# Head norms of both token tiles in two phases, and a new order of the memory's first norms, in a two-layer hybrid attention kernel

## The chip, the cores and the metric

The kernel runs on one core of a Trainium2 chip. The metric is the time of one execution on the device in microseconds, the median of several runs. Five engines work side by side: TensorE (PE, and PEld for its weight loads), VectorE (DVE), ScalarE (ACT), GpSimd (POOL) and SyncE (SP, which only issues DMAs).

## The reference

Two layers of attention on 256 tokens of width 1024, all in fp32. In each layer the rows of x are normed and multiplied by `w_in`, which gives queries, keys, values and gates of three branches: six heads of causal attention (the "a" columns; with 256 tokens its block selection falls away), six heads of dilated attention (the "b" columns) and four heads that look at 256 rows of a memory (the "m" columns). The memory's keys and values are the normed memory rows times `w_mem_kv`. Every head of queries and keys, 64 wide, is normed with a gain of its own; the a and b heads are also rotated by position:

```
qa = rope(rms_norm(to_heads(a_q), qk_g[0])); ka = rope(rms_norm(to_heads(a_k), qk_g[1]))
qb, kb: the same with qk_g[2], qk_g[3]
mkv = rms_norm(mem, mem_norm_g) @ w_mem_kv
qm = rms_norm(to_heads(m_q), qk_g[4]); km = rms_norm(to_heads(m_k), qk_g[5])
y = concat([oa * silu(a_g), ob * silu(b_g), om * silu(m_g)]);  x = x + y @ w_out
```

## The kernel before

**Tiling.** The 256 tokens (and the 256 memory rows) are two tiles of 128, t = 0 and 1. Every weight is brought from memory in fp32 into a buffer `raw` (three of these) and split into `hi`, a rounded copy (ACT, line 429), and `lo`, the rest (DVE, line 430), of which five each are held. Each product is three matmuls: hi·xmh, hi·xml, lo·xmh, where xmh and xml are the same split of the activations. A piece of a weight that is split at once is called a part; the parts are numbered from 0 in the order mkv (0 to 3), mq (4, 5), mg (6, 7), bq (8 to 11), bk (12 to 15) and so on. The variable `ahead` says how many parts beyond the one that is multiplied next are already split in program order.

**PSUM.** Four banks `acc` go round among the projections, two for each: mkv has the first two, mq the other two, mg the first two again, bq those of mq. A projection can start on a bank only when all that reads the one before it is done. Three banks `wk` serve transposes and scores, and one, `o`, the attention's output.

**Order.** The order of PE's instructions is written out by hand: a projection is a list of steps, and between them a small planner with a clock of estimated costs puts in the transposes, scores and outputs of heads that are due (`poll`, `spawn`; the `D_` constants are the delays that it plans with). While `pinning[0]` is set, which lasts from the start until the memory's keys of layer 0 are normed, DVE, ACT, POOL and the DMA queue keep program order too. After that the library's scheduler orders these engines by its own costs, with program order as the priority.

**The norm of heads** (`normed`, lines 256 to 276) takes one accumulator of one tile: ACT squares it (260), DVE sums over each head (262), DVE multiplies by 1/64 and adds epsilon (154), POOL raises to the power -1/2 (155), DVE multiplies the accumulator by the gain or by gain times cosine (266); for a and b DVE also multiplies the swapped halves by gain times sine (271) and adds (275); last, DVE multiplies by the head's factor (276). It is called for t = 0, then for t = 1, and each call ends before the next begins in program order.

**Layer 0 around the memory** (lines 553 to 579). mkv is computed from memory rows that carry no factor yet. After mq's first step ACT copies mkv to `kv`; after mq's fourth step the first memory tile's row factor is made (a Square over 1024 columns with a sum, ACT 160; DVE 154; POOL 155). At mq's first part the parts 6 and 7 are split, at its second part 8. Then come the norms of mq for both tiles, the second memory tile's row factor, two DMAs (the constants and the other gains), and for each tile a multiplication of `kv` by its row factor (573) and the norm of its keys. Line 515 multiplies the gain of the memory's queries, of both layers, by 0.125 on POOL. Then POOL makes the tables of gains times cosine and sine (203 to 208), PE runs mg, and bq follows. The transposes of the memory's queries and keys (PE, line 113) are planned into bq.

Of the kernel before, what the change touches and what calls it, by code (L numbers as in the profile page):

```python
# [25 lines left out]
SPLIT_BUFS = 5  # L26
# [40 lines left out]
def hybrid_kernel(ctx: ExitStack, tc: tile.TileContext, x, mem, mem_t, gains, w_in, w_out, w_mem_kv, qk_g, const, out):  # L67
    nc = tc.nc
    cp = ctx.enter_context(tc.tile_pool(name="cp", bufs=1))
    wp = ctx.enter_context(tc.tile_pool(name="wp", bufs=2))  # L70
    sp = ctx.enter_context(tc.tile_pool(name="sp", bufs=2))
# [17 lines left out]
    def pin(ins):  # L89

        return tc.keep_in_program_order(ins) if pinning[0] else ins
# [142 lines left out]
    def project_t(xs, chunk, n):  # L234

        accs = [acc_p.tile([P, 512], F32, tag="acc", name="acc")[:, :T] for _ in range(n // P)]

        def steps():
            for k0, nk, w in chunk:
                for k in range(nk):  # L240
                    products([(acc, k0 + k, [x[:, k0 + k] for x in xs], [p[:, k, e * P:(e + 1) * P] for p in w])
                              for e, acc in enumerate(accs)], 0, KD - 1, x_moves=True)
                    yield

        return accs, steps()

    def run(projection):
        accs, steps = projection
        for _ in steps:
            poll()  # L250
        return accs

    def heads(v):
        return v.rearrange("p (h d) -> p h d", d=HD)

    def normed(acc, n, dst, tables):

        h = n // HD
        sq = sp.tile([P, n], F32, tag="sq", name="sq", bufs=2)
        pin(nc.scalar.activation(sq, acc, AF.Square))  # L260
        ss = sp.tile([P, h], F32, tag="hss", name="hss", bufs=4)
        pin(nc.vector.tensor_reduce(ss, heads(sq), axis=AX.X, op=ALU.add))  # L262
        rs = sp.tile([P, h], F32, tag="hrs", name="hrs", bufs=4)
        rsqrt(rs, ss, h, 1.0 / HD)
        t1 = sp.tile([P, n], F32, tag="t1", name="t1", bufs=2)
        pin(nc.vector.tensor_tensor(heads(t1), heads(acc), tables[0][:, None, :].to_broadcast([P, h, HD]),
                                    op=ALU.mult))
        if len(tables) > 1:
            t2 = sq
            half = dict(s=2, d=HD // 2)  # L270
            pin(nc.vector.tensor_tensor(t2.rearrange("p (h s d) -> p h s d", **half),
                                        acc.rearrange("p (h s d) -> p h s d", **half)[:, :, ::-1, :],
                                        tables[1].rearrange("p (s d) -> p s d", s=2)[:, None]
                                        .to_broadcast([P, h, 2, HD // 2]), op=ALU.mult))
            pin(nc.vector.tensor_tensor(t1, t1, t2, op=ALU.add))
        pin(nc.vector.tensor_tensor(heads(dst), heads(t1), rs.unsqueeze(2).to_broadcast([P, h, HD]), op=ALU.mult))  # L276

    live = dict(pr=0, pT=0, o=0, heads=0, pairs=0, s=0, t=0, v=0)

# [84 lines left out]
    for side in "ab":  # L364
        c = in_cols[side + "g"][0]
# [69 lines left out]
    def weights():  # L435

        i = at[0]
        at[0] += 1
        while at[1] < len(splits) and units[splits[at[1]][0]][0] == i:
            s = at[1]  # L440
            at[1] += 1
            split(s + ahead[0])
            yield splits[s][1], splits[s][2], parts[s]
# [37 lines left out]
    for l in range(DEPTH):  # L481
# [3 lines left out]
        if l == 0:  # L485

            mem_xs = xm_tiles()
            first = sp.tile([P, WHOLE, T], F32, tag="v", name="whole", bufs=2)
            mkv, steps = project(mem_xs, weights(), 512)
            r_mem = []  # L490
            g = gT[:, 16:24]
            for k in range(WHOLE):

                whole[k] = first[:, k]
                pin(nc.vector.tensor_scalar(whole[k], memT[:, k], g[:, k:k + 1], None, op0=ALU.mult))
                next(steps)
            for k2 in range(WHOLE, KD - 2, 2):
                split_x(mem_xs, memT[:, k2:k2 + 2], g, k2)
                split(k2 // 2 + 1)
                next(steps)  # L500
            turned = [(o_p.tile([P, 2 * T], F32, tag="o", name="o") if k2 == 6 else work()).rearrange(
                "p (a t q) -> p a t q", a=2, t=NT) for k2 in range(0, KD, 2)]
            for t in range(NT):
                normed_rows(t, xn)
                for k in range(KD):
                    transpose(turned[k // 2][:, k % 2, t], xn[:, t, k * P:(k + 1) * P])
            split_x(mem_xs, memT[:, KD - 2:KD], g, KD - 2)
            split(KD // 2)
            next(steps)
            for k2, v in zip(range(0, KD, 2), turned):  # L510
                split_x(xs, v.rearrange("p a t q -> p a (t q)"), gx, k2)
                if k2 < 4:
                    split(SPLIT_BUFS + k2 // 2)
            mem_gain = gB[:, :, 4]
            pin(nc.gpsimd.tensor_scalar(mem_gain, mem_gain, 0.125, None, op0=ALU.mult))
            ahead[0] = SPLIT_BUFS - 1
        else:
            mkv, steps = project(mem_xs, weights(), 512)
            for t in range(NT):
                normed_rows(t, xn)  # L520
            for k in range(KD):
                next(steps)
                if k >= KD // 2:
                    split_x(xs, transposed(xn, 2 * k - KD), gx, 2 * k - KD)
# [4 lines left out]
        def gates(accs, dst):  # L529
            for e, acc in enumerate(accs):  # L530
                th = sp.tile([P, T], F32, tag="th", name="th", bufs=2)
                nc.scalar.activation(th, acc, AF.Tanh, scale=0.5)
                nc.vector.scalar_tensor_tensor(dst[:, e], th, 1.0, acc, op0=ALU.add, op1=ALU.mult)
# [23 lines left out]
        for i, _ in enumerate(steps):  # L557
# [4 lines left out]
            if i == 3 and l == 0:  # L562
                mem_junk = sp.tile([P, D], F32, tag="v", name="mem_junk", bufs=2)
                r_mem.append(row_scale(mem_sb, 0, "rmem", mem_junk))
        for t, acc in enumerate(mq):
            normed(acc, 256, qn[:, t], [gB[:, l, 4]])
        if l == 0:
            r_mem.append(row_scale(mem_sb, 1, "rmem", mem_junk))
            pin(nc.sync.dma_start(cst, const))
            load_gains(0, 4)  # L570
        for t in range(NT):
            if l == 0:
                pin(nc.scalar.activation(kv[:, t], kv[:, t], AF.Copy, scale=r_mem[t]))
            normed(kv[:, t, 0:256], 256, kn[:, t], [gB[:, l, 5]])
        pinning[0] = False
        start_heads(2, 6, qn, kn, None, v, gate, ready, D_NORM + D_MEM)
        tab = prepare_tables(l)
        gates(run(project_t(xs, weights(), 256)), gate)
        ready["gate"] = clock[0] + D_EVAC

        for kind, e0 in ((2, 3), (0, 0)):
            if kind == 2:
                masks = [cst[:, C_DIL:C_DIL + 128], cst[:, C_DIL + 128:C_DIL + 384]]
            else:
                masks = [cst[:, C_CAUSAL + 128:C_CAUSAL + 256], cst[:, C_CAUSAL:C_CAUSAL + 256]]
            if l + 1 < DEPTH and kind == 0:
                mem_xs = xm_tiles()
                spawn(next_mem(mem_xs, gT[:, 24 + 8 * l:32 + 8 * l]), D_FIRST_MEM)
            qn, kn, v, gate = head_tiles(384, 384)
            ready = dict(v=1e9, gate=1e9)  # L590
            for i, dst in ((0, qn), (1, kn)):
                for t, acc in enumerate(run(project(xs, weights(), 384))):
                    normed(acc, 384, dst[:, t], (tab[:, kind + i, 0, t], tab[:, kind + i, 1, t]))
            start_heads(3, e0, qn, kn, masks, v, gate, ready)
            for t, acc in enumerate(run(project(xs, weights(), 384))):
                nc.scalar.copy(v[:, t], acc)
            ready["v"] = clock[0] + D_EVAC
            gates(run(project_t(xs, weights(), 256)), gate[:, 0:2])
            gates(run(project_t(xs, weights(), 128)), gate[:, 2:3])
            ready["gate"] = clock[0] + D_EVAC  # L600
# [64 lines left out]
```

## Time and profile before

| | |
|---|---|
| Runs | 294.54, 295.4 and 712.39 us; median 295.4 us |
| Profiled execution | 294.36 us, of which the span from the first to the last instruction is 292.6 us |
| Busy in the span | PE 285.8 us, PEld 250.6, DVE 204.3, ACT 200.0, POOL 53.8 |
| TensorE clock granted | full, in every slice |
| DMA | 47.33 MB, mean 162 GB/s |

A row of the timeline gives the start in us from the span's start, the time, the engine, the line, the operation, what it writes and reads, how many instructions were merged into the row, and in brackets how long the engine had been idle before, and what ended that. PE's ends are modelled, since matmuls are pipelined; their starts are what was recorded. ACT and DVE may start an instruction before the one ahead has ended.

### The profile page before, as it was taken

Reading aid. Unit: us, or ns where it says so; the run is one execution under the profiler, and the core shown is the slowest. Engines: PE = TensorE matmul, PEld = TensorE weight load, DVE = VectorE, ACT = ScalarE, POOL = GpSimd, SP = SyncE. Lnnn points to the kernel's source line nnn. Section 1 sums busy time; section 2 is a strip of 40 time slices with the busy share of each in tenths; the row PEclk is TensorE's granted clock in tenths of the full one; section 3 lists DMA queues with packets and bytes.
Section 4 is the critical chain, followed back from the end, with each engine's and each line's share of the span. In section 5 each row is a group of like instructions: output and inputs, shape, how many; then the busy total and the mean of one; then the engine's idle time right before and its main releaser. Section 6 shows DMA issues by size and latency. Waiting matters only on the chain.

```text
span 292.6 us, 4974 instructions
## 1 busy us (share of the span) xinstructions
PE 285.8 (98%) x1810; PEld 250.6 (86%) x1810; DVE 204.3 (70%) x456; ACT 200.0 (68%) x445; POOL 53.8 (18%) x73
## 2 busy tenths in 40 slices
PE   8999889999999999999999999999999999999994
PEld 5699879889988999877788999989899899987773
DVE  1696889796557997755585577979655699765413
ACT  2997858785798747978375655868588864698600
POOL 0103596030002130000011049703000123000000
PEclk9999999999999999999999999999999999999999
DMA  7999565609227046646106727560913715820003
GB/s 236 389 367 373 184 182 186 179 2 319 57 71 237 19 155 262 196 162 224 65 19 233 225 101 195 168 179 2 298 38 109 239 52 165 316 81 36 3 0 143
DMA packets 32793, 47.33 MB, mean 162 GB/s; under 512 B 1280, under 2 KB 27648, under 8 KB 32768
## 3 DMA queue, kind: packets, MB, share of 16 engines
q1 hardware_dynamic: 32336, 46.22, 48.5%
q10 hardware_dynamic: 432, 0.79, 0.8%
q8 instruction: 14, 0.23, 0.3%
q14 instruction: 11, 0.09, 0.1%
HBM read 45.96 MB, written 1.05 MB: 161 GB/s over the span
## 4 chain that ended last, share of the span: by engine, by line
PE 86%; DMA 7%; DVE 3%; POOL 1%; issue 1%; ACT 1%; SPq 0%; DVEq 0%; ACTq 0%
PE acc L110 68%; PE wk L113 7%; PE wk L110 5%; PE o L110 5%; DMA raw<-in_w_in_dram 3%; DMA x_sb<-in_x_dram 2%; DVE lo L430 1%; DMA raw<-in_w_mem_kv_dram 1%; POOL hrs L155 1%; DVE hss L262 0%; ACT xn L160 0%; POOL r L155 0%; DVE ms L154 0%; DVE kn L276 0%; ACT hi L429 0%
## 5 line engine op out<-in xcount | busy, mean ns | idle before, releaser
L430 DVE TENSOR_TENSOR lo<-raw,hi 128x768 fp32r<-128x768 f32 (+1 forms) x91 | 97.4, 1089 | 34.1 <-ACT hi L429 33.4
L429 ACT CAST hi<-raw 128x768 fp32r<-128x768 f32 (+1 forms) x91 | 83.8, 937 | 31.2 <-PE acc L110 22.7
L110 PE MATMUL acc<-hi,xmh 128*128 128x384 f32 (+2 forms) x252 | 67.3, 349 | 0.8 <-ACT hi L429 0.8
L110 PE MATMUL acc<-hi,xml 128*128 128x384 f32 (+2 forms) x252 | 63.6, 335 | 0.0
L110 PE MATMUL acc<-lo,xmh 128*128 128x384 f32 (+2 forms) x252 | 63.6, 335 | 0.0
L155 POOL TENSOR_TENSOR hrs<-ms,mhalf 128x6 f32<-128x6 f32 (+1 forms) x24 | 30.1, 1255 | 121.2 <-DVE ms L154 120.8
L110 PEld LDWEIGHTS acc<-hi,xmh 128*128 128x128 f32 x252 | 42.7, 189 | 6.3 <-issue 3.0
L110 PEld LDWEIGHTS acc<-lo,xmh 128*128 128x128 f32 x252 | 45.0, 188 | 1.2
L110 PEld LDWEIGHTS acc<-hi,xml 128*128 128x128 f32 x252 | 44.9, 188 | 1.2
L110 PE MATMUL acc<-hi,yT 128*128 128x512 f32 x128 | 41.0, 402 | 0.0
L110 PE MATMUL acc<-xmh,hi 128*128 128x256 f32 x128 | 29.7, 293 | 0.0
L340 ACT ACTIVATE pr<-pr,nm 128x128 f32<-128x128 f32 (+1 forms) x48 | 21.4, 447 | 11.1 <-DVE nm L338 10.9
L110 PE MATMUL acc<-xmh,lo 128*128 128x256 f32 x128 | 28.4, 283 | 0.0
L110 PE MATMUL acc<-xml,hi 128*128 128x256 f32 x128 | 28.4, 283 | 0.0
L110 PEld LDWEIGHTS acc<-hi,yT 128*128 128x128 f32 x128 | 23.0, 188 | 4.9 <-issue 0.7
L346 ACT ACTIVATE pr<-pr,rinv 128x128 f32<-128x128 f32 (+1 forms) x64 | 25.8, 462 | 0.2 <-DVE rinv L344 0.2
L110 PE MATMUL acc<-lo,yT 128*128 128x512 f32 x64 | 25.0, 391 | 0.0
L110 PEld LDWEIGHTS acc<-xmh,hi 128*128 128x128 f32 x128 | 20.9, 191 | 0.7 <-issue 0.7
L110 PEld LDWEIGHTS acc<-xml,hi 128*128 128x128 f32 x128 | 21.0, 191 | 0.0
L110 PEld LDWEIGHTS acc<-xmh,lo 128*128 128x128 f32 x128 | 21.0, 191 | 0.0
L357 ACT COPY pT<-wk 128x384 f32<-128x384 f32 (+1 forms) x32 | 15.5, 504 | 5.1 <-PE wk L113 5.1
L338 DVE CUSTOM_DVE_ANT_0 pr<-wk,cst 128x128 f32<-128x128 f32 (+1 forms) x48 | 14.2, 352 | 3.0 <-PE wk L110 3.0
(76 smaller groups left out, 355.3 us busy)
## 6 DMA issues: line engine op xcount, KB each, us to landing
raw<-in_w_in_dram SPq DMA_DIRECT2D x24, 768.0 KB, 4.8
raw<-in_w_in_dram SPq DMA_DIRECT2D x7, 1024.0 KB, 5.4
raw<-in_w_out_dram SPq DMA_DIRECT2D x6, 1024.0 KB, 4.9
raw<-in_w_in_dram SPq DMA_DIRECT2D x6, 512.0 KB, 3.7
raw<-in_w_out_dram SPq DMA_DIRECT2D x4, 512.0 KB, 4.2
raw<-in_w_mem_kv_dram SPq DMA_DIRECT2D x2, 1024.0 KB, 5.3
raw<-in_w_mem_kv_dram SPq DMA_DIRECT2D x2, 512.0 KB, 6.5
x_sb<-in_x_dram SPq DMA_DIRECT2D x2, 512.0 KB, 6.7
```

The source lines that it names most:

```text
L110: pe(nc.tensor.matmul(out, a, b, start=start, stop=stop), us)
L113: pe(nc.tensor.transpose(out, a, ident), 0.109)
L155: pin(nc.gpsimd.tensor_tensor(dst, ms, mhalf[:, :n], op=ALU.pow))
L338: nc.vector.tensor_tensor_reduce(out=pr[:, spans[t]], in0=s[:, spans[t]], in1=masks[t], scale=-1.0, scalar=3e38, op0=ALU.add, op1=ALU.min, ...
L340: nc.scalar.activation(pr[:, spans[t]], pr[:, spans[t]], AF.Exp, scale=-1.0, bias=nm[:, t:t + 1], accum_out=sums[:, t:t + 1])
L346: nc.scalar.activation(pr[:, spans[t]], pr[:, spans[t]], AF.Copy, scale=rinv[:, t:t + 1])
L357: nc.scalar.copy(pT[:, :n], ps[:, :n])
L429: pin(nc.scalar.copy(hi, raw))
L430: pin(nc.vector.tensor_tensor(lo, raw, hi.bitcast(F32), op=ALU.subtract))
```

## The change

`normed` now takes both tiles' accumulators. For each tile it squares, sums, makes the factor and does the multiplications that read the accumulator; what is left, the add and the multiplication by the factor, is a function `rest` that is called later, for both tiles. The 0.125 moves from POOL's multiplication of the gain into the multiplication of the accumulator, which becomes a scalar_tensor_tensor.

In layer 0 `ahead` is smaller by one until mq's norms are issued: part 7 is split at mq's second part and not at its first, and part 8 is issued behind mq's first phase. There follow, in program order: the second memory row factor, squares and sums of the unscaled keys, and for each tile the square of the row factor over 64, the head's factor from it, and one part's split (8, then 9); then `rest` of mq's norms, the two DMAs, and for each tile the two multiplications that make the keys, the first with the row factor. The memory's values get their row factor after mg's gates, outside the pinned stretch.

```
-    def normed(acc, n, dst, tables):
+    def head_squares(acc, n):
         sq = sp.tile([P, n], F32, tag="sq", name="sq", bufs=2)
         pin(nc.scalar.activation(sq, acc, AF.Square))
...
+        return sq, ss
+    def head_scale(ss, n, scale):
+        rs = sp.tile([P, n // HD], F32, tag="hrs", name="hrs", bufs=4)
+        rsqrt(rs, ss, n // HD, scale)
+        return rs
+    def normed(accs, n, dsts, tables, scale=None):
...
+        for t, acc in enumerate(accs):
+            t2, ss = head_squares(acc, n)
+            rs = head_scale(ss, n, 1.0 / HD)
...
+            if scale is None:
+                pin(nc.vector.tensor_tensor(heads(t1), heads(acc), first, op=ALU.mult))
+            else:
+                pin(nc.vector.scalar_tensor_tensor(heads(t1), heads(acc), scale, first, op0=ALU.mult, op1=ALU.mult))
+            if len(tables) > 1:
+                pin(nc.vector.tensor_tensor(t2..., acc..., tables[1][t]..., op=ALU.mult))
+            held.append((t1, t2, rs))
+        def rest():
+            for (t1, t2, rs), dst in zip(held, dsts):
+                if len(tables) > 1:
+                    pin(nc.vector.tensor_tensor(t1, t1, t2, op=ALU.add))
+                pin(nc.vector.tensor_tensor(heads(dst), heads(t1), rs..., op=ALU.mult))
+        return rest
...
-            mem_gain = gB[:, :, 4]
-            pin(nc.gpsimd.tensor_scalar(mem_gain, mem_gain, 0.125, None, op0=ALU.mult))
-            ahead[0] = SPLIT_BUFS - 1
+            ahead[0] = SPLIT_BUFS - 2
...
-        for t, acc in enumerate(mq):
-            normed(acc, 256, qn[:, t], [gB[:, l, 4]])
+        rest = normed(mq, 256, [qn[:, t] for t in range(NT)], [[gB[:, l, 4]] * NT], 0.125)
+        keys = [kv[:, t, 0:256] for t in range(NT)]
         if l == 0:
+            ahead[0] = SPLIT_BUFS - 1
             r_mem.append(row_scale(mem_sb, 1, "rmem", mem_junk))
+            sums = [head_squares(k, 256)[1] for k in keys]
+            scales = []
+            for t in range(NT):
+                r2 = sp.tile([P, 1], F32, tag="r2", name="r2", bufs=2)
+                pin(nc.vector.tensor_scalar(r2, r_mem[t], r_mem[t], 1.0 / HD, op0=ALU.mult, op1=ALU.mult))
+                scales.append(head_scale(sums[t], 256, r2))
+                split(at[1] + t + 3)
+            rest()
             pin(nc.sync.dma_start(cst, const))
             load_gains(0, 4)
-        for t in range(NT):
-            if l == 0:
-                pin(nc.scalar.activation(kv[:, t], kv[:, t], AF.Copy, scale=r_mem[t]))
-            normed(kv[:, t, 0:256], 256, kn[:, t], [gB[:, l, 5]])
+            for t in range(NT):
+                t1 = sp.tile([P, 256], F32, tag="t1", name="t1", bufs=2)
+                pin(nc.vector.scalar_tensor_tensor(heads(t1), heads(keys[t]), r_mem[t], gB[:, l, 5]..., op0=ALU.mult, op1=ALU.mult))
+                pin(nc.vector.tensor_tensor(heads(kn[:, t]), heads(t1), scales[t]..., op=ALU.mult))
+        else:
+            rest()
+            normed(keys, 256, [kn[:, t] for t in range(NT)], [[gB[:, l, 5]] * NT])()
...
         gates(run(project_t(xs, weights(), 256)), gate)
+        if l == 0:
+            for t in range(NT):
+                nc.scalar.activation(v[:, t], v[:, t], AF.Copy, scale=r_mem[t])
...
-                for t, acc in enumerate(run(project(xs, weights(), 384))):
-                    normed(acc, 384, dst[:, t], (tab[:, kind + i, 0, t], tab[:, kind + i, 1, t]))
+                accs = run(project(xs, weights(), 384))
+                normed(accs, 384, [dst[:, t] for t in range(NT)],
+                       [[tab[:, kind + i, c, t] for t in range(NT)] for c in range(2)])()
```

## Rows read from the trace of the kernel before

**Rows 1.** The page: busy time of the engines, share of the span, instructions.

```profile
PE 285.8 (98%) x1810; PEld 250.6 (86%) x1810; DVE 204.3 (70%) x456; ACT 200.0 (68%) x445; POOL 53.8 (18%) x73
```

**Rows 2.** Busy time by stretch (start:end of the stretch and its length, then each engine's busy us and instructions, the clock, the DMA share, GB/s).

```profile
9.00:25.00 16.00, 16.00 (x100) 14.17 (x100) 14.29 (x23) 15.06 (x27) 2.30 (x3) 1.00 1.07 375
25.00:43.00 18.00, 16.29 (x113) 15.45 (x113) 13.30 (x30) 12.13 (x22) 10.85 (x14) 1.00 0.69 220
43.00:178.00 135.00, 135.00 (x871) 119.42 (x868) 98.84 (x223) 95.90 (x216) 21.90 (x31) 1.00 0.47 150
178.00:289.00 111.00, 110.90 (x713) 96.72 (x712) 75.41 (x176) 73.82 (x177) 18.10 (x22) 1.00 0.40 128
```

**Rows 3.** What PE waited for, two of four rows (the other two lie in the first 5 us): us in total, times, longest.

```profile
PE wk L113 <- DVE kn L276: 0.9, 1, 0.9
PE acc L110 <- ACT hi L429: 0.8, 1, 0.8
```

**Rows 4.** PE's timeline, from mg's part 7 into bq.

```profile
28.51 0.40 PE L110 MATMUL acc<-xmh,lo 128*128 128x256 f32 x2
...
30.91 0.34 PE L110 MATMUL acc<-hi,xmh 128*128 128x384 f32 x1
32.01 0.41 PE L110 MATMUL acc<-hi,xmh 128*128 128x384 f32 x1 [0.77 <-ACT hi L429]
...
32.61 0.51 PE L110 MATMUL acc<-lo,xmh 128*128 128x384 f32 x2
...
34.69 0.51 PE L110 MATMUL acc<-lo,xmh 128*128 128x384 f32 x2
...
37.22 0.27 PE L113 MATMUL wk<-ident,kn 128*128 128x128 f32 x1
37.33 0.27 PE L113 MATMUL wk<-ident,qn 128*128 128x128 f32 x1
38.55 0.33 PE L113 MATMUL wk<-ident,kn 128*128 128x128 f32 x1 [0.95 <-DVE kn L276]
```

**Rows 5.** DVE's timeline in that stretch.

```profile
22.85 2.34 DVE L430 TENSOR_TENSOR lo<-raw,hi 128x1024 fp32r<-128x1024 f32 x2
...
28.84 0.41 DVE L262 TENSOR_REDUCE hss<-sq 128x4 f32<-128x256 f32 x1
...
29.36 0.42 DVE L266 TENSOR_TENSOR t<-acc,gB 128x256 f32<-128x256 f32 x1
...
31.45 0.42 DVE L266 TENSOR_TENSOR t<-acc,gB 128x256 f32<-128x256 f32 x1
31.78 0.94 DVE L430 TENSOR_TENSOR lo<-raw,hi 128x768 fp32r<-128x768 f32 x1
...
38.03 0.46 DVE L276 TENSOR_TENSOR kn<-t,hrs 128x256 f32<-128x256 f32 x1
```

**Rows 6.** ACT's timeline in that stretch.

```profile
20.94 2.04 ACT L429 CAST hi<-raw 128x1024 fp32r<-128x1024 f32 x2
...
23.79 1.12 ACT L160 ACTIVATE mem_junk<-mem_sb 128x1024 f32<-128x1024 f32 x1
24.73 0.26 ACT L160 ACTIVATION_READ_ACCUMULATOR mem_junk<-mem_sb 128x1 f32 x1
27.09 0.83 ACT L429 CAST hi<-raw 128x768 fp32r<-128x768 f32 x1 [2.10 <-DMA raw<-in_w_in_dram]
27.83 0.65 ACT L260 ACTIVATE sq<-acc 128x256 f32<-128x256 f32 x2
...
29.41 0.72 ACT L573 ACTIVATE v<-v,rmem 128x512 f32<-128x512 f32 x1
...
34.57 0.42 ACT L260 ACTIVATE sq<-v 128x256 f32<-128x256 f32 x1
```

**Rows 7.** POOL's timeline: the gain's multiplication, factors, and the tables' first products.

```profile
23.82 1.77 POOL L515 TENSOR_SCALAR gB<-gB 128x128 f32<-128x128 f32 x1 [9.02 <-DMA gB<-in_qk_g_dram]
31.61 1.01 POOL L155 TENSOR_TENSOR hrs<-ms,mhalf 128x4 f32<-128x4 f32 x1 [1.07 <-DVE ms L154]
33.23 0.56 POOL L155 TENSOR_TENSOR rmem<-ms,mhalf 128x1 f32<-128x1 f32 x1 [0.60 <-DVE ms L154]
...
39.51 1.03 POOL L208 TENSOR_TENSOR tab<-gB,cst 128x64 f32<-128x64 f32 x1
...
42.79 0.32 POOL L208 TENSOR_TENSOR tab<-gB,cst 128x64 f32<-128x64 f32 x1
```

**Rows 8.** The DMA queue: the memory rows' transfer in us to landing (it was issued at 11.22), and when the transfer of bk's first half and the four after it began to be issued.

```profile
mem_sb<-in_mem_dram SPq DMA_DIRECT2D x1, 1024.0 KB, 12.1
25.21 17.54 SPq L408 DMA_DIRECT2D raw<-in_w_in_dram  x5
```

**Rows 9.** Groups of DVE instructions between 25 and 43 us: busy us, mean ns of one.

```profile
L533 DVE SCALAR_TENSOR_TENSOR gate<-th,acc 128x256 f32<-128x256 f32 x2 | 0.8, 410 | 0.0
L154 DVE TENSOR_SCALAR ms<-ss 128x1 f32<-128x1 f32 x2 | 0.3, 144 | 0.0
```

**Rows 10.** DVE and PE where layer 0's aq is normed: its wide operations, the split of av's first part, and that part's first product with lo.

```profile
94.37 0.55 DVE L262 TENSOR_REDUCE hss<-sq 128x6 f32<-128x384 f32 x1
98.83 1.82 DVE L430 TENSOR_TENSOR lo<-raw,hi 128x768 fp32r<-128x768 f32 x2
100.37 0.51 PE L110 MATMUL acc<-lo,xmh 128*128 128x384 f32 x2
```

More of the change, by code (lines that the diff above doesn't have):

```diff
@@ L254, in heads @@
         return v.rearrange("p (h d) -> p h d", d=HD)
-    def normed(acc, n, dst, tables):
-        h = n // HD
+    def head_squares(acc, n):
         sq = sp.tile([P, n], F32, tag="sq", name="sq", bufs=2)
         pin(nc.scalar.activation(sq, acc, AF.Square))
-        ss = sp.tile([P, h], F32, tag="hss", name="hss", bufs=4)
+        ss = sp.tile([P, n // HD], F32, tag="hss", name="hss", bufs=4)
         pin(nc.vector.tensor_reduce(ss, heads(sq), axis=AX.X, op=ALU.add))
[L263 to L276, printed above, removed]
@@ new lines, in head_squares @@
+        return sq, ss
[4 more added lines that the diff above has]
+    def normed(accs, n, dsts, tables, scale=None):
+        h = n // HD
+        half = dict(s=2, d=HD // 2)
+        held = []
+        for t, acc in enumerate(accs):
+            t2, ss = head_squares(acc, n)
+            rs = head_scale(ss, n, 1.0 / HD)
+            t1 = sp.tile([P, n], F32, tag="t1", name="t1", bufs=2)
+            first = tables[0][t][:, None, :].to_broadcast([P, h, HD])
+            if scale is None:
[3 more added lines that the diff above has]
+            if len(tables) > 1:
+                pin(nc.vector.tensor_tensor(t2.rearrange("p (h s d) -> p h s d", **half),
+                                            acc.rearrange("p (h s d) -> p h s d", **half)[:, :, ::-1, :],
+                                            tables[1][t].rearrange("p (s d) -> p s d", s=2)[:, None]
+                                            .to_broadcast([P, h, 2, HD // 2]), op=ALU.mult))
+            held.append((t1, t2, rs))
[3 more added lines that the diff above has]
+                    pin(nc.vector.tensor_tensor(t1, t1, t2, op=ALU.add))
+                pin(nc.vector.tensor_tensor(heads(dst), heads(t1), rs.unsqueeze(2).to_broadcast([P, h, HD]),
+                                            op=ALU.mult))
+        return rest
@@ L564, in hybrid_kernel @@
                 r_mem.append(row_scale(mem_sb, 0, "rmem", mem_junk))
-        for t, acc in enumerate(mq):
-            normed(acc, 256, qn[:, t], [gB[:, l, 4]])
+        rest = normed(mq, 256, [qn[:, t] for t in range(NT)], [[gB[:, l, 4]] * NT], 0.125)
+        keys = [kv[:, t, 0:256] for t in range(NT)]
         if l == 0:
+            ahead[0] = SPLIT_BUFS - 1
             r_mem.append(row_scale(mem_sb, 1, "rmem", mem_junk))
+            sums = [head_squares(k, 256)[1] for k in keys]
[6 more added lines that the diff above has]
+            rest()
             pin(nc.sync.dma_start(cst, const))
             load_gains(0, 4)
-        for t in range(NT):
-            if l == 0:
-                pin(nc.scalar.activation(kv[:, t], kv[:, t], AF.Copy, scale=r_mem[t]))
-            normed(kv[:, t, 0:256], 256, kn[:, t], [gB[:, l, 5]])
+            for t in range(NT):
+                t1 = sp.tile([P, 256], F32, tag="t1", name="t1", bufs=2)
+                pin(nc.vector.scalar_tensor_tensor(heads(t1), heads(keys[t]), r_mem[t],
+                                                   gB[:, l, 5][:, None, :].to_broadcast([P, 4, HD]),
+                                                   op0=ALU.mult, op1=ALU.mult))
+                pin(nc.vector.tensor_tensor(heads(kn[:, t]), heads(t1),
+                                            scales[t].unsqueeze(2).to_broadcast([P, 4, HD]), op=ALU.mult))
+        else:
+            rest()
+            normed(keys, 256, [kn[:, t] for t in range(NT)], [[gB[:, l, 5]] * NT])()
         pinning[0] = False
```

## The prediction

> **What bounds the kernel now.** I read the page first, then busy time by stretch, then PE's waits, then the timelines around each wait. The page has PE busy for 285.8 of 292.6 us [rows 1]. By stretch, PE is busy for all of 9 to 25 us, all of 43 to 178 and 110.90 of 111 to 289, at the full clock; only 25 to 43 lacks some: 16.29 of 18 [rows 2]. PE's own waits agree: beside the start-up there are two, 0.9 us for `kn` and 0.8 us put down to a cast [rows 3]. So the sum is short: what this change can win lies in those two places, and what it can lose is a new wait of PE anywhere.
>
> The timeline sizes them better than modelled ends do, by starts. In bq, products follow each other every 0.17 us (12 in 32.61 to 34.69), but between the first and the second lie 1.10 us: 0.93 lost. Transposes follow every 0.11 us, but 37.33 to 38.55 is 1.22: 1.11 lost [rows 4]. Together 2.04 us.
>
> What ends them? The first is named after the cast at 27.09, which was long done, so it was another: bq's second tile takes the bank of mq's second accumulator, and the multiplication that last reads it ran from 31.45 to 31.87 [rows 5]; PE went on at 32.01. It came so late because three things stand in a row. ACT, which keeps order, waited 2.10 us for the weights of part 8, with mq's squares queued behind that cast [rows 6]. Then DVE took the split of part 8 and tile 0, waiting for POOL's power, before tile 1. The second wait is plain: the second `kn` ended at 38.49 [rows 5], and PE moved at 38.55.
>
> **The change, part by part.** I lay the new order out with durations of the same rows.
>
> *ACT.* Part 7's cast leaves its place ahead of the first row factor (1.02 us, half of the pair at 20.94) and stands behind it. The row factor then starts when the memory rows have landed, 11.22 + 12.1 = 23.3, not at 23.79 [rows 6, 8]; with Square and read it ends near 24.4. Part 7's cast: 24.4 to 25.4. mq's accumulators are finished at about 25.2 (bq's start, 30.91, less mg's 48 products of 0.12 us), so the two squares run at 25.4 to 26.0, 2.4 us sooner than at 27.83. The second row factor follows to 27.1, the keys' squares to 28.3 (the second needs a `sq` buffer that DVE frees at 27.9), the casts of parts 8 and 9 to 29.9. The 2.1 us wait for the weights is gone: they land at 27.09, ahead of their new place.
>
> *DVE.* Part 7's `lo` (half of 2.34 us) runs 25.5 to 26.6. A tile's first phase takes 0.9 us (28.84 to 29.78 in rows 5), two take until 28.4. So the banks come free at 28.4, and bq's second tile wants them at 31.08: 2.7 us spare, **0.93 us won**. Then reduces, squares of factors and `ms` to 29.3, part 8's `lo` (0.94) to 30.2, part 9's to 31.4, `rest` and the keys, six operations of about 0.42 us issued every 0.35, to 33.5. PE wants the last `kn` at 37.44 - 0.93 = 36.5: 3.0 us spare, **1.11 us won**.
>
> *POOL.* Line 515 goes (1.77 us), hidden before, as nothing waits on it. The powers, four of 1.01 and one of 0.56 [rows 7], stand at 27.3 to 32.1; the second row factor at 29.9 is what part 9's `lo` may wait for. The tables start at 32, 6 us sooner.
>
> *The casts that were moved past.* Part 7's `lo` is wanted at 28.51, done at 26.6. Part 8's is wanted at 32.61 - 0.93 = 31.7, done at 30.2. Part 9's is wanted at 33.8, done at 31.4 [rows 4]. Spare 1.9, 1.5 and 2.4 us. These are what hides the longer queue ahead of them; past that, each late us is a lost us of PE.
>
> *SP.* Nothing changes order. bk's first transfer waits for the buffer that part 7's `lo` frees, so it is issued near 26.6, not 25.21 [rows 8]; its `lo` is needed 11 us after bq starts, so I cost it at nothing. The two small DMAs, for constants and gains, keep their place.
>
> *Operations that the trace lacks.* The multiplications with three inputs: nearest a row of 0.41 us for that form at 256 columns [rows 9]; bounds 0.41 and 0.55, the wide ones of rows 10; I take 0.42, and the upper end adds 0.5 us to the keys, inside 3.0 spare. The factor's square, 128x1: 0.14 [rows 9] to 0.41; twice the upper end, 0.5 us, stays within part 8's 1.5. The values' scaling, half of line 573's 0.72 or all of it, lies on ACT some 20 us ahead of its use. None reaches PE at either end, and a gain beyond the two waits is excluded: PE has no other idle time there.
>
> *The twelve later norms* do the same operations in another order. Banks come free sooner, but no row shows PE waiting for one, so I put the gain at 0. The scheduler's new order may delay a cast. The tightest that I found is av's first part in layer 0: its `lo` ends at 98.83 + 0.95 = 99.78, and PE reads it at 100.37 [rows 10], 0.59 us spare. Three wide operations of the second tile now stand ahead of the first tile's end, 3 x 0.55 = 1.65 us; so the cost lies between 0 and 1.06 us. I take 0, as the same work has to be done by then in both orders.
>
> **The sum.** The profiled execution is 294.36 us, 1.8 of it outside the span. 294.36 - 2.04 = 292.3. It stands 1.0 below the median of the runs shown and 0.2 below the lowest; the same sum from the median is 293.4. I say **292.7 us**.
>
> **The rivals.**
>
> *A new wait at a later cast* (0.13). As above, up to 1.06 us back: 293.4 from the profiled execution. For it: 0.59 us spare, on an engine that is full there. Against: the first tile's end waits for POOL's power anyway, and the scheduler can put a split into that wait.
>
> *Only the bank's wait goes* (0.08). The keys end after 36.5 because their chain, ACT to DVE to POOL to DVE, is longer than laid out by over 3 us: 294.36 - 0.93 = 293.4 or less of a gain. Against: the spare time.
>
> *The waits move* (0.05). What follows 43 us is as late as before because something else sets it, bk's weights or scores: 294.4. Against: PE is busy in all of 43 to 178, so what comes sooner stays sooner.
>
> *POOL and DVE shut each other out* (0.05), the slow side. The tables' products take 1.03 us beside splits and 0.32 without them [rows 7], so the two engines do meet. If each POOL instruction held DVE off for its whole time, the powers up to part 8's `lo` (2.0 + 0.6) would end it at 32.8, 1.1 late, and with the other two powers and four table products (2.0 + 1.3) the last `kn` would end near 39.4, 0.9 after its old 38.49: 295.3 us, slower. It decides from `kn` at 38.5. Against it stands a pair of rows: the power from 31.61 to 32.62 and the split from 31.78, whose 0.94 us are what splits take elsewhere [rows 5, 7]; they overlapped in full. The Trainium skill has this as a rule (SBUF — State Buffer, "Who interferes with whom"): a port pair is shared by GpSimd and a DVE instruction with two SBUF inputs, whoever starts first has it for the whole instruction, and the other is blocked. By that rule the time would be this rival's; the powers here do not follow it and the table products may, so the measurement decides.
>
> **How the numbers follow.** The forecast has 0.69. Its own range is 292.0 (the sum, and the runs' lower edge) to 293.5 (the sum from the median). The range goes on to 294.6, so that it takes in the bound of the later cast, a half gain and an unchanged profiled execution: 291.9 to 294.6. Two per cent, 5.9 us, is about what a measurement of this kernel can tell from no change. PE's idle time between 9 and 289 us is 1.8 us by modelled ends, so faster by that is as good as excluded: 0.01. Slower by 5.9 us takes several waits like those that went: 0.02. Within: 0.97.
>
> **What would show it.** In the profile after: mq's two squares near 25.5 and ahead of a cast 768 wide; both first-phase multiplications done by 29; bq's products every 0.17 us from the first; the last `kn` before 35 and its transposes 0.11 apart; PE waiting for nothing between 9 and 289 us; a span near 290.6. It would be wrong if PE waits for `lo` of parts 8 or 9, if `kn` ends behind its transposes, or if a wait of over 0.5 us appears around 98 to 101 us.

## The result, and the profile after

The changed kernel takes 292.26 us, the median of 8 runs (292.11 to 293.14), beside 294.5 us for the kernel before on the same chip: a ratio of 0.9935, 95% interval 0.9915 to 0.9955. The forecast was 292.7 us, its bare sum 292.3. The span fell from 292.6 to 290.3 us.

The page's first part after, to be read beside [rows 1]: PE has 1.0 us less of modelled busy time (part of a wait counts as busy there: [rows 4] give 0.77 us idle where the starts lose 0.93), the other engines nearly what they had.

```profile
PE 284.8 (98%) x1810; PEld 250.0 (86%) x1810; DVE 205.0 (71%) x458; ACT 199.9 (69%) x445; POOL 54.3 (19%) x72
```

Busy time by stretch after, columns as in [rows 2], the stretches cut where the same work stands now, some 2 us sooner. The stretch that lacked 1.71 us of PE lacks nothing; what the last one lacks lies behind PE's last product.

```profile
25.00:41.00 16.00, 16.00 (x114) 15.63 (x114) 15.03 (x31) 12.17 (x23) 13.84 (x19) 1.00 0.75 244
41.00:176.00 135.00, 135.00 (x872) 119.38 (x869) 99.00 (x223) 96.10 (x216) 21.07 (x25) 1.00 0.46 151
176.00:287.00 111.00, 110.66 (x712) 96.49 (x711) 75.13 (x176) 74.01 (x177) 17.60 (x22) 1.00 0.40 129
```

All that PE waited for after. These rows lie in the first 11 us; both rows of [rows 3] are gone.

```profile
PE warm L120 <- DVE mhalf L83: 1.0, 1, 1.0
PE acc L110 <- ACT hi L449: 0.3, 1, 0.3
PE acc L110 <- DVE whole L515: 0.2, 1, 0.2
```

PE's timeline after, the products and transposes of [rows 4]. The wait ahead of bq's second product is gone (two products from 31.03, the next pair 0.35 later), and the last key's transpose follows the one before it by 0.11 us.

```profile
31.03 0.52 PE L110 MATMUL acc<-hi,xmh 128*128 128x384 f32 x2
...
31.73 0.51 PE L110 MATMUL acc<-lo,xmh 128*128 128x384 f32 x2
...
33.81 0.51 PE L110 MATMUL acc<-lo,xmh 128*128 128x384 f32 x2
...
36.45 0.27 PE L113 MATMUL wk<-ident,qn 128*128 128x128 f32 x1
36.56 0.27 PE L113 MATMUL wk<-ident,kn 128*128 128x128 f32 x1
```

ACT's timeline after [rows 6]: row factor, part 7's cast, mq's squares, and only then part 8's cast, which no longer waits 2.10 us for its weights.

```profile
23.57 1.06 ACT L160 ACTIVATE mem_junk<-mem_sb 128x1024 f32<-128x1024 f32 x1 [0.41 <-DMA mem_sb<-in_mem_dram]
...
24.63 1.03 ACT L449 CAST hi<-raw 128x1024 fp32r<-128x1024 f32 x1
25.57 0.65 ACT L259 ACTIVATE sq<-acc 128x256 f32<-128x256 f32 x2
...
28.47 2.29 ACT L449 CAST hi<-raw 128x768 fp32r<-128x768 f32 x3
```

DVE's timeline after [rows 5]: the second tile's multiplication out of PSUM, the splits of parts 8, 9 and 10, the multiplications of the two keys (601, then 604) with a gate in between, and, later, bq's first product with a table, which waits for nothing.

```profile
28.22 0.42 DVE L282 SCALAR_TENSOR_TENSOR t<-acc,gB 128x256 f32<-128x256 f32 x1
...
29.64 0.95 DVE L450 TENSOR_TENSOR lo<-raw,hi 128x768 fp32r<-128x768 f32 x1
...
30.89 0.95 DVE L450 TENSOR_TENSOR lo<-raw,hi 128x768 fp32r<-128x768 f32 x1
...
32.44 0.48 DVE L601 SCALAR_TENSOR_TENSOR t<-v,rmem,gB 128x256 f32<-128x256 f32 x1
32.83 0.99 DVE L450 TENSOR_TENSOR lo<-raw,hi 128x768 fp32r<-128x768 f32 x1
33.75 0.54 DVE L604 TENSOR_TENSOR kn<-t,hrs 128x256 f32<-128x256 f32 x1
34.21 0.54 DVE L601 SCALAR_TENSOR_TENSOR t<-v,rmem,gB 128x256 f32<-128x256 f32 x1
34.67 0.41 DVE L551 SCALAR_TENSOR_TENSOR gate<-th,acc 128x256 f32<-128x256 f32 x1
35.01 0.49 DVE L604 TENSOR_TENSOR kn<-t,hrs 128x256 f32<-128x256 f32 x1
...
41.28 0.55 DVE L280 TENSOR_TENSOR t<-acc,tab 128x384 f32<-128x384 f32 x1
```

POOL's timeline after [rows 7]: the keys' two powers, and the start of layer 0's tables.

```profile
30.02 2.69 POOL L155 TENSOR_TENSOR hrs<-ms,mhalf 128x4 f32<-128x4 f32 x2
32.69 0.46 POOL L203 TENSOR_SCALAR gB<-gB 128x64 f32<-128x64 f32 x1
```

To see where time is won and lost, I compare one matmul's start in two traces; all kernels here issue the same 1810 matmuls in the same order. After minus before, from one execution of each: +0.15 at 16.9 us of the old span, -0.80 at bq's second product (32.0), -1.99 at the last key's transpose (38.55), -2.13 at 53.5, -2.24 at the last matmul. Both gains are where they were forecast, and they stay. The timed medians carry the size: these are single executions.

### The profile page after: what moved, and what is told of

The parts are those of the page before. It is cut to its first block, busy times and chain, and to the rows that moved or that the text cites. A ratio compares the mean times of both kernels' runs of the same rounds, so it can differ in the third digit from the quotient of the medians.

```text
span 290.3 us, 4967 instructions
## 1 busy us (share of the span) xinstructions
PE 284.8 (98%) x1810; PEld 250.0 (86%) x1810; DVE 205.0 (71%) x458; ACT 199.9 (69%) x445; POOL 54.3 (19%) x72
## 3 DMA queue, kind: packets, MB, share of 16 engines
HBM read 45.96 MB, written 1.05 MB: 162 GB/s over the span
## 4 chain that ended last, share of the span: by engine, by line
PE 93%; DMA 3%; DVE 1%; ACT 0%; POOL 0%; SPq 0%; issue 0%; DVEq 0%
PE acc L110 76%; PE wk L113 8%; PE wk L110 5%; PE o L110 5%; DMA x_sb<-in_x_dram 2%; DMA raw<-in_w_mem_kv_dram 1%; DVE xn L491 0%; ACT xn L160 0%; POOL r L155 0%; SPq L428 0%; DVE x_sb L669 0%; SPq L98 0%; DVEq L699 0%; DVE ms L154 0%; PE o L113 0%
## 5 line engine op out<-in xcount | busy, mean ns | idle before, releaser
L155 POOL TENSOR_TENSOR hrs<-ms,mhalf 128x6 f32<-128x6 f32 (+1 forms) x24 | 30.2, 1262 | 118.0 <-DVE ms L154 117.5
L110 PE MATMUL acc<-xml,hi 128*128 128x256 f32 x128 | 28.4, 283 | 0.0
```

The costliest lines, as they stand in the source:

```text
L110: pe(nc.tensor.matmul(out, a, b, start=start, stop=stop), us)
```

## The experiments

The theory to be tested: two waits of PE went, through three edits (the two phases, the queries ahead of part 8's cast, the keys' new form), and what PE does sooner stays sooner. The rival: something behind them takes the gain back. The table gives, for each kernel, PE's starts minus those of the kernel before at five matmuls, by their us in the old span; the change from 16.9 us to the end (the first 10 us depend on when the first transfers land and vary by up to 2 us between executions of the same code); and the timed medians and ratio.

| kernel | 16.9 | 32.0 | 38.6 | 48.0 | 53.5 | end | end less 16.9 | us | before | ratio |
|---|---|---|---|---|---|---|---|---|---|---|
| changed | 0.15 | -0.80 | -1.99 | -2.08 | -2.13 | -2.24 | -2.39 | 292.26 | 294.5 | 0.9935 |
| e1 two phases alone | 0.36 | -0.57 | -0.47 | -0.47 | 0.17 | 0.21 | -0.15 | 294.84 | 294.17 | 1.0023 |
| e2 queries first alone | 0.26 | -0.66 | -0.18 | -0.19 | 0.62 | 0.63 | 0.37 | 295.18 | 294.17 | 1.0028 |
| e3 keys' form alone | 1.93 | 1.12 | 0.79 | 0.76 | 1.68 | 1.58 | -0.35 | 295.41 | 294.17 | 1.0038 |
| e4 changed, old keys | -0.17 | -1.09 | -2.27 | -2.35 | -1.92 | -1.92 | -1.75 | 293.55 | 294.17 | 0.9970 |
| changed again | -0.05 | -0.97 | -2.16 | -2.24 | -2.29 | -2.39 | -2.34 | 292.45 | 294.48 | 0.9935 |
| e6 changed, tables late | 0.52 | -0.43 | -1.61 | -1.70 | -0.58 | -0.58 | -1.10 | 293.83 | 294.48 | 0.9982 |
| e7 e1, bq's tables first | 0.66 | -0.27 | -0.59 | -0.62 | -0.67 | -0.67 | -1.33 | 294.30 | 294.48 | 1.0001 |
| e8 changed, bq's tables first | 0.41 | -0.51 | -1.70 | -1.78 | -1.83 | -1.94 | -2.35 | 292.72 | 294.48 | 0.9939 |
| e5 changed, wide norms by tile | 1.95 | 1.03 | -0.15 | -0.23 | -0.28 | -0.35 | -2.30 | 292.80 | 294.51 | 0.9941 |
| e9 before, bq's tables first | 0.32 | -0.26 | -0.26 | -0.27 | -0.32 | -0.32 | -0.64 | 294.23 | 294.51 | 0.9994 |
| e10 e4, bq's tables first | 1.21 | 0.28 | -0.89 | -0.95 | -0.99 | -0.99 | -2.20 | 292.88 | 294.51 | 0.9938 |
| e11 changed, cast first | 0.07 | -0.73 | -0.93 | -0.99 | -1.05 | -0.99 | -1.06 | 293.38 | 294.51 | 0.9955 |

### One part alone, or one part undone

**e1**, the kernel before with all norms in two phases:

```
+    def normed(accs, n, dsts, tables, scale=None):
...
-        for t, acc in enumerate(mq):
-            normed(acc, 256, qn[:, t], [gB[:, l, 4]])
+        rest = normed(mq, 256, [qn[:, t] for t in range(NT)], [[gB[:, l, 4]] * NT])
+        rest()
```

> The kernel before with the two phases alone: all norms of heads take both tiles at once, mq's included, but mq's squares stay behind the cast of part 8, POOL still multiplies the gain, and the keys still get their row factor from ACT first. Theory (two waits of PE, 0.93 us for mq's bank and 1.11 us for the last kn, each of them with a place of its own in layer 0): the second tile's multiplication ends near 30.6, ahead of 31.08, so the bank's wait goes; but kn still hangs on the second row factor (ACT's scaling near 33, then both tiles' norms) and ends near 37.5 where PE wants it at 36.5, so a wait of 0.9 to 1.2 us stays there. Gain 0.8 to 1.1 us against the kernel before (about 293.5 us if that is 294.4). Rival (it is the early reading of PSUM in all norms that gains, by banks that come free sooner): the whole 2.1 us, 292.3 us, and PE's starts shift by small steps all over the two layers.

**e2**, the kernel before with the new place of the casts:

```
-            ahead[0] = SPLIT_BUFS - 1
+            ahead[0] = SPLIT_BUFS - 2
...
+            ahead[0] = SPLIT_BUFS - 1
             r_mem.append(row_scale(mem_sb, 1, "rmem", mem_junk))
+            split(at[1] + 3)
```

> The kernel before with the order of casts alone: part 7's cast one step later, mq's norms (still tile by tile) ahead of part 8's cast, keys in the old form. Theory: mq's squares near 25.5 and the second tile's multiplication done by 30, so the bank's wait of 0.93 us goes; part 8's lo stands behind the whole norm of both tiles and ends near 32.0 where PE wants it at 31.7, a new wait of 0.1 to 0.5; kn ends near 37.3, wanted at 36.8, a wait of 0.3 to 0.7 stays. Gain 1.0 to 1.5 us. Rival (two phases are what frees the bank): no gain, 294.4.

**e3**, the kernel before with squares and sums of unscaled keys, `r2`, and the keys multiplied by factor and gain at once:

```
+                pin(nc.vector.tensor_scalar(r2, r_mem[t], r_mem[t], 1.0 / HD, op0=ALU.mult, op1=ALU.mult))
...
-                pin(nc.scalar.activation(kv[:, t], kv[:, t], AF.Copy, scale=r_mem[t]))
-            normed(kv[:, t, 0:256], 256, kn[:, t], [gB[:, l, 5]])
+                pin(nc.vector.scalar_tensor_tensor(heads(t1), heads(keys[t]), r_mem[t], ...
```

> The kernel before with the keys' new form alone: squares and sums of unscaled keys, the row factor in the head's factor and in the last multiplications, the values scaled later; mq's norms and the casts where they were. Theory: the bank's wait of 0.93 us stays as it is; kn ends near 37.5 where PE wants it at 37.44, so at most 0.3 us of that wait stays; part 9's lo stands behind the keys' sums and ends near 34.9, wanted at 34.69, a new wait of 0 to 0.4. Gain 0.6 to 1.1 us. Rival (keys follow mq's norms, so their own form gives nothing): kn as late as before, no gain.

**e4**, the changed kernel with the keys' old form (the inverse of e3's diff, with one split call left for part 8).

> The changed kernel with the keys in the old form again (ACT multiplies keys and values by the row factor, then the two-phase norm of both tiles). Theory: mq's part alone brings everything behind it forward by over 2 us, so kn ends near 35.6, ahead of 36.5, and both waits are gone without the new form: 292.3 us, the same as the changed kernel within 0.3. Rival (the new form is what saves the kn wait of 1.11 us): 293.4 us.

All four missed. e1 to e3 were to be 0.6 to 1.5 us faster and are slower: intervals 1.0011 to 1.0035, 1.0015 to 1.0041, 1.0027 to 1.0049. e4 was to be like the changed kernel and keeps less than half of the gain (0.9956 to 0.9984). The table says where the gain goes: in all four PE has won something by 48 us, and between 48.0 and 53.5 it loses 0.64, 0.81, 0.92 and 0.43 us. The changed kernel loses nothing there. This accounts for the missing gain in the traces of e1 and e3 (-0.15 and -0.35 are left), but not for medians that are 0.7 and 1.2 us longer than before; see the end of this section.

What stands at that place? In the kernel before, DVE's timeline from 43 us shows bq's first product waiting for a table, and the maxima of the memory's heads (`nm`) queued behind it (DVE's timeline, then PE's):

```profile
44.43 0.56 DVE L266 TENSOR_TENSOR t<-acc,tab 128x384 f32<-128x384 f32 x1 [0.99 <-POOL tab L206]
...
44.98 1.28 DVE L331 TENSOR_REDUCE nm<-wk 128x2 f32<-128x512 f32 x2
```

```profile
49.86 1.03 PE L113 MATMUL wk<-ident,pr 128*128 128x128 f32 x8
```

Exponentials, sums and the scaling of the probabilities follow from `nm`, and PE's transposes `wk<-ident,pr` start at 49.86 in that trace, without a wait. DVE's wait for the table cost PE nothing there. A PE that comes sooner meets it. In e1's timeline of DVE, PE comes 0.47 us sooner and the table does not:

```profile
44.69 0.56 DVE L280 TENSOR_TENSOR t<-acc,tab 128x384 f32<-128x384 f32 x1 [1.33 <-POOL tab L206]
```

In e4 (DVE's timeline) PE comes 2.3 us sooner and the table 1.9:

```profile
42.51 0.56 DVE L280 TENSOR_TENSOR t<-acc,tab 128x384 f32<-128x384 f32 x1 [0.78 <-POOL tab L206]
```

In e3 it waits longest, since one POOL instruction ahead of the tables took 4.91 us in place of 0.37 (POOL's timeline, then DVE's):

```profile
38.09 4.91 POOL L203 TENSOR_SCALAR gB<-gB 128x64 f32<-128x64 f32 x1
```

```profile
39.21 3.55 DVE L430 TENSOR_TENSOR lo<-raw,hi 128x768 fp32r<-128x768 f32 x4
...
46.13 0.56 DVE L266 TENSOR_TENSOR t<-acc,tab 128x384 f32<-128x384 f32 x1 [1.93 <-POOL tab L206]
```

So there is a third place, behind the two. The tables are made in the order aq, ak, bq, bk, though bq is first to use one. In the changed kernel POOL begins them at 32.69 and not at about 38, and bq's product at 41.28 waits for nothing. The next runs test that.

### The third place

**The changed kernel again**, beside the following three:

> The changed kernel as it is, so that the next three can be held against it on the same chip. Every theory: about 2.0 us under the kernel before, 292.1 to 292.7 us.

It repeats: 0.9918 to 0.9951.

**e6**, the changed kernel with POOL kept busy ahead of layer 0's tables:

```
...
+            for _ in range(5):
+                tc.keep_in_program_order(nc.gpsimd.tensor_tensor(idle, idle, mhalf[:, :4], op=ALU.pow))
```

> The changed kernel with five powers of 1.01 us on POOL, of a tile that nothing reads, ahead of layer 0's tables: it takes back alone that POOL gets to the tables sooner. Theory of a third place (the first parts showed gains that were lost again at 50 us: bq's norm on DVE waits for POOL's tables, with the maxima of the memory's heads queued behind it, then exponentials, and PE's transposes of the probabilities): bq's table comes near 44.2 instead of 39.9, the maxima start near 44.7 instead of 41.7, and PE's transposes, due at 47.8 to 48.3, wait 1.2 to 1.8 us; 293.5 to 294.1 us. Rival (only the two waits for mq's bank and the keys decide, as I predicted): the same time as the changed kernel within 0.3.

Its time is in the expected window (0.9968 to 0.9995), and 1.12 us of PE go between 48.0 and 53.5. Beside the splits the five powers took 7.25 us together and not 5 x 1.01. DVE's and PE's timelines show the chain, PE's wait for `pr` at its end; by starts the eight transposes take 1.57 us up to the next product, in the kernel before 0.79:

```profile
43.92 0.56 DVE L280 TENSOR_TENSOR t<-acc,tab 128x384 f32<-128x384 f32 x1 [2.19 <-POOL tab L206]
...
44.40 1.28 DVE L351 TENSOR_REDUCE nm<-wk 128x2 f32<-128x512 f32 x2
```

```profile
49.02 0.95 PE L113 MATMUL wk<-ident,pr 128*128 128x128 f32 x4 [0.27 <-ACT pr L366]
```

**e7**, e1 with one line more, and **e8**, the changed kernel with that line:

```
-        for kind in range(4):
+        for kind in (2, 3, 0, 1):
```

> The two phases alone (e1) with POOL's tables in another order: bq's and bk's, which are used first, ahead of aq's and ak's. Theory of a third place: bq's table is there near 40, DVE's 1.3 us wait for it at 44.7 goes, so the 0.6 us that e1 lost at 50 us come back; its own kn wait stays. 0.4 to 0.8 us under e1 as it was measured (294.84), so 294.0 to 294.4, and in the trace PE's start at 53 us lies as far ahead of the kernel before as at 38. Rival (what e1 lost is another order of DVE or ACT in bq's norm): no difference from e1.

> The changed kernel with the tables in that order. Theory: with the whole change nothing waits for the tables any more, and PE is full behind them, so 0 to 0.2 us under the changed kernel. Rival (tables still hold the softmax a little, by the 0.1 us that PE's starts drift in 50 to 53 us): the same number; a difference over 0.4 us would speak for a place that I haven't seen.

Both come out as expected. e7 loses nothing after 38.6, and bq's product waits for nothing (DVE's timeline):

```profile
43.15 0.54 DVE L280 TENSOR_TENSOR t<-acc,tab 128x384 f32<-128x384 f32 x1
```

Its ratio is 0.9984 to 1.0018, 0.22% under e1's; that difference is no larger than the noise of the two ratios taken together, so it is the trace that shows the place. For e8 (0.9925 to 0.9953) the line does nothing clear of noise, as there the tables come in time anyway.

**e9**, the kernel before with the same line, and **e10**, e4 with it:

> The kernel before, with the tables of layer 0 made in the order bq, bk, aq, ak and nothing else changed. Theory (the third place lies hidden behind PE's two waits there): DVE's wait of 0.99 us for the table at bq's first product goes, PE's two waits of about 1 us stay, and the time is the same, 0 +- 0.3 us to the kernel before. Rival (the table is itself on the path that sets the end before): 0.5 us or more faster.

> The changed kernel with the keys in their old form (the run before of that edit lost 0.34 us of its 2.27 us at the third place, PE's start at 50 to 53 us) and the tables in the order bq, bk, aq, ak. Theory (the new form of the keys is worth only that POOL comes to the tables sooner): the 0.3 us come back, PE's lead at 53 us is that at 38 us, and the time is within 0.4 us of the changed kernel, 292.3 to 292.9. Rival (the keys' form is worth something by itself): the time stays at about 293.5, a ratio of 0.997.

e9 is the kernel before (0.9979 to 1.0009): the third place is hidden there. DVE's product starts at 43.09 without waiting, and the wait for the last key is 1.11 us again. But bq's wait for the bank, in code that is the same, is smaller in this execution (PE's timeline, to be read beside [rows 4]):

```profile
31.22 0.34 PE L110 MATMUL acc<-hi,xmh 128*128 128x384 f32 x1
31.75 0.41 PE L110 MATMUL acc<-hi,xmh 128*128 128x384 f32 x1 [0.19 <-ACT hi L429]
```

0.53 less 0.17 is 0.36, where I had taken 0.93: here PE began 0.3 us later and part 8's weights landed 0.3 us sooner (its cast starts at 26.82, not 27.09). In e3, where mq's norms and the casts are also in the order of before and PE began 1.9 us later, the wait is 0.11 (the second product starts 0.28 us behind the first), so 0.82 of the 1.17 us that e3 has won by 48 us are not from its edit. One profile of before gave one draw of that wait.

e10 has 0.9916 to 0.9960, and its lead at 53.5 is that at 38.6, as the theory said: with the queries ahead of the cast and the tables in bq's order, the old keys are as good as the new ones. What the keys' new form brings there is that POOL is done with their powers sooner (at 32.71 us, in e4 at 35.42).

### The two remaining edits

**e5**, the changed kernel with the norms of a and b called for one tile at a time:

```
-                normed(accs, 384, [dst[:, t] for t in range(NT)],
-                       [[tab[:, kind + i, c, t] for t in range(NT)] for c in range(2)])()
+                for t in range(NT):
+                    normed(accs[t:t + 1], 384, [dst[:, t]], [[tab[:, kind + i, c, t]] for c in range(2)])()
```

> The changed kernel with the wide norms of a and b (tiles of 384 columns) called tile by tile again; only mq's norm, the narrow ones, keeps its two phases. Theory (the order of the tiles in the wide norms costs and brings nothing, since PE has other work until the later one is done): 0 +- 0.3 us to the changed kernel, so 292.1 to 292.8. Rival (the two phases in the later norms carry part of the gain, or take some of it away): more than 0.5 us off, with a new or a vanished wait of PE in the layers.

As expected (0.9923 to 0.9959; from 16.9 us on its trace gains 2.30, the changed kernel's 2.39): the two phases are worth nothing in the wide norms.

**e11**, the changed kernel with part 8's cast ahead of mq's squares:

```
-            ahead[0] = SPLIT_BUFS - 2
+            ahead[0] = SPLIT_BUFS - 1
...
-            ahead[0] = SPLIT_BUFS - 1
```

> The changed kernel with the cast of part 8 ahead of mq's squares again. Theory (the two phases and the keys leave enough room): mq's squares begin near 27.8 instead of 25.6 us, the multiplication out of the second accumulator ends near 30.6, still ahead of where PE wants the bank (31.1), so the first wait stays away; the last key comes near 36.7, where PE wants it at 36.5, and the tables some 1.6 us later: 0 to 0.6 us over the changed kernel, 292.4 to 293.0. Rival (the order of cast and queries is what frees the bank): the wait of 0.9 us is back and the time is 293.2 or more.

Missed: 293.38 us (0.9938 to 0.9971), by the ratios 0.6 us over the changed kernel and by the traces 1.3: the time that the rival gave, but not by its mechanism. The bank's wait is 0.16 us (the second product starts 0.33 us behind the first in place of 0.17), nearly gone, as the theory had it. The keys are late (PE's timeline, then ACT's):

```profile
36.74 0.27 PE L113 MATMUL wk<-ident,qn 128*128 128x128 f32 x1
37.62 0.33 PE L113 MATMUL wk<-ident,kn 128*128 128x128 f32 x1 [0.60 <-DVE kn L603]
```

```profile
27.59 0.83 ACT L449 CAST hi<-raw 128x768 fp32r<-128x768 f32 x1 [1.04 <-DMA raw<-in_w_in_dram]
28.33 0.65 ACT L259 ACTIVATE sq<-acc 128x256 f32<-128x256 f32 x2
```

The weights landed at 27.59 in this execution, so the squares began at 28.33 and not at 27.8; the last key ended at 37.07 + 0.48 = 37.55, 0.85 later than I had put it, and PE lost 0.88 - 0.11 = 0.77 us. So the queries' place ahead of the cast is worth some 0.6 to 1.3 us, most of it through the keys behind them.

What stays open: the times of e1, e3, e4 and e7 lie 0.8 to 1.6 us above what their traces gain from 16.9 us on, the others' by -0.1 to 0.6. The traces show one execution each (those of e4 and e7 the fastest of their twelve), the first 10 us and the bank's wait vary, and no run separates these. So it stays open why e1 to e3 are slower than the kernel before, and whether the keys' new form is worth something where the cast comes first: e11 is 0.46% faster than e7 by the ratios, but gains 0.27 us less by the traces. No run takes mq's two phases alone out of the changed kernel, either; the nearest is e2, in whose trace PE waits 0.4 us for part 8's `lo` and its wait for the last key grows from 1.11 to 1.27. The places are shown by the traces; the sizes are taken from the timed runs.

## Why the prediction came out as it did

**The two waits: right.** bq's second tile finds its bank free: the last multiplication out of it ended at 28.22 + 0.42 = 28.64, forecast 28.4. PE's shift grows by 0.92 us there and by 1.11 at the last key, the two terms of the sum. That the first term was one draw (0.93 there, 0.36 in e9, 0.11 in e3) I could not know from one trace, so that the bare sum met the measured time is in part luck; the medians differ by 2.24 us in the first measurement and by 2.03 when the changed kernel ran again.

**The laid-out order: right until the splits.** Row factor 23.57 (forecast 23.3), part 7's cast until 25.66 (25.4), mq's squares until 26.22 (26.0), part 8's `lo` done at 30.59 (30.2), part 9's at 31.84 (31.4), tables from 32.69 (32). The multiplications with three inputs took 0.42 us out of PSUM, as taken, and 0.48 and 0.54 for the keys. The scheduler put the scaling of the first tile's values on ACT at 27.15 (0.50 us), ahead of the keys' squares, where the layout had none.

**The last key: the step that was mis-sized.** I had it at 33.5 with 3.0 us spare, and "before 35" among the signs. It ended at 35.01 + 0.49 = 35.50, and PE used it at 36.56: 1.06 us spare. Two things were left out. The scheduler put part 10's `lo` and a gate between the keys' operations; by the starts in the rows above they cost 0.92 and 0.34 us. And the keys' operations ran beside POOL's tables, where the last three took 0.54, 0.54 and 0.49 us; in e6, where powers stand there, 0.42, 0.48 and 0.43. The rest is part 9's `lo`, done at 31.84 and not at 31.4. The keys' two powers took 2.69 us, not 2 x 1.01, but the second was done at 32.71, long before its use at 35.01: that put off the tables and not the key. With a spare of 1.06 instead of 3.0, the 2 us by which the key is later in e11 (37.55 for 35.50) were enough to bring the wait back.

**The later norms at nothing: right**, by e5. The tightest cast, av's first part, kept its spare time; DVE's row for its split, the first of three, and PE's for its first product with `lo`:

```profile
96.72 2.68 DVE L450 TENSOR_TENSOR lo<-raw,hi 128x768 fp32r<-128x768 f32 x3
```

```profile
98.22 0.51 PE L110 MATMUL acc<-lo,xmh 128*128 128x384 f32 x2
```

96.72 + 0.95 leaves 0.55 us, where it had been 0.59 [rows 10].

**"PE is busy in all of 43 to 178, so what comes sooner stays sooner": wrong**, and it was the whole case against the rival that the waits move. A PE without idle time shows only that nothing is late at its present pace. e1 to e4 were late by 0.43 to 0.92 us as soon as PE came sooner, and e6 put that place back into the changed kernel for 1.1 us. The row that told it was in the trace of before: DVE idle 0.99 us for a table, with PE's next inputs queued behind. The result held because the change also frees POOL 5 us sooner; I had "The tables start at 32, 6 us sooner" in the text and gave it no worth. That the gain stayed was luck as far as the prediction goes.

**POOL and DVE: my reading against that rival covered one case of two, and its outcome did not come.** I said that the powers do not follow the rule of mutual exclusion, because one that ran from 31.61 overlapped a split from 31.78 in full [rows 5, 7]. In that case the power had begun first. e6 shows the other case: a power and a split that both begin at 33.19, POOL's row and then DVE's:

```profile
33.19 1.81 POOL L615 TENSOR_TENSOR idle<-idle,mhalf 128x4 f32<-128x4 f32 x1
```

```profile
33.19 0.95 DVE L450 TENSOR_TENSOR lo<-raw,hi 128x768 fp32r<-128x768 f32 x1
```

The split takes its 0.95 us and ends at 34.14; the power ends 0.86 later, at 35.00. So it is nearly throughout: in all these traces 15 powers of 128x4 began between 25 and 42 us while a split ran. 14 ended 0.86 or 0.87 us after that split, where one that begins alone takes 1.01; the fifteenth began 0.12 us before the split's end and took its 1.01. In the changed kernel that is 0.4 us for one of the keys' powers and 0.3 for the other. The Trainium skill's rule (SBUF — State Buffer, "Who interferes with whom") is that a DVE instruction with two SBUF inputs contends with a GpSimd instruction that reads SBUF, and that the order of issue decides which of them blocks. The traces agree with it for a power that begins behind a split. They do not agree for the reverse: a split that begins 0.17 us behind a power takes 0.94 [rows 5, 7], so a power does not hold DVE for its whole time, which is what my slow rival needed.

## What to carry to other kernels

A bottleneck engine with no gaps does not prove that a gain upstream will stay: look at the engines that feed it for waits that its present lateness hides, above all a wait on an in-order engine with the bottleneck's next inputs queued behind it. Where parts of a change do nothing alone and together work, look for a place behind them that one part happens to clear, and test it by delaying that place alone. A spare time that is laid out from durations needs the instructions that a scheduler may still put in between, and the stretched durations beside other engines.

## What the hardware showed that I had not expected

POOL can be held off for several DVE instructions on end. The tensor_scalar of 128x64 in e3 began 0.09 us into a split and took 4.91 us, until a key's multiplication and four more splits had gone by; in the kernel before and in e4 the same instruction takes 0.37. Table products do get in between two splits, at 1.03 us each in place of 0.32 [rows 7], and so does a second such tensor_scalar in the changed kernel, which began at 37.92 among five splits and took 1.07. Why one gets in and another doesn't, no run here separates.

The wait for the bank in the unchanged code was 0.93 us in one execution, 0.36 in another and 0.11 in a third; between the first two lie 0.3 us in the landing of one transfer and 0.3 in PE's start. A term of that kind wants more than one trace.
